# One MLP layer by seven block products instead of eight, in a two-layer hybrid inference step

## The chip, the core and the metric

The kernel runs on one core of a Trainium2 chip. The core has four compute engines, each with its own instruction stream that is worked off in order: TensorE (PE in the profile; its weight loads are shown apart as PEld), VectorE (DVE), ScalarE (ACT) and GpSimd (POOL). Transfers from memory are issued by a fifth stream, SyncE (SP). The metric is the device time of one execution in microseconds (us); lower is better.

## What is computed

The kernel is one inference step of a model with two layers (DEPTH = 2) over 640 tokens: 512 latent tokens and 128 context tokens, each with its own modulation vectors. Everything is float32. Each layer mixes tokens by four head groups and then runs a squared-ReLU MLP with 1024 features and 4096 hidden units:

```python
def squared_relu_mlp(h, w1, w2):
    return jnp.square(jax.nn.relu(h @ w1)) @ w2

def modulate(x, g, shift, scale):
    return rmsnorm(x, g) * (1 + scale) + shift

def trunk_layer(x, mod, p, mix_fn):
    shift1, scale1, gate1, shift2, scale2, gate2 = jnp.split(mod, N_MOD, axis=-1)
    y, ctx_state = mix_fn(modulate(x, p['norm1'], shift1, scale1))
    x = x + gate1 * y
    x = x + gate2 * squared_relu_mlp(modulate(x, p['norm2'], shift2, scale2), p['w1'], p['w2'])
    return x, ctx_state
```

The vectors in `mod` are products of the two groups' conditioning vectors with a weight matrix of 1024 by 6144 per layer; the kernel calls this part "ada".

## The kernel before

Features lie on the 128 partitions and tokens on the free axis, in two halves of 384 and 256 tokens (`HALVES`). Each float32 operand is held as a high and a low part, and every product is three matmuls: high by high, high by low, low by high (`mm3`, L241 to L243).

**Weights.** `load_unit` (L228) brings a unit of [128, 1024] floats: SP issues a transfer of 512 KB into one of three `raw` buffers, ACT casts it to the high part of one of four `hl` buffers (L232), and VectorE subtracts to get the low part (L233). With `pool=True` GpSimd does that subtraction; the first MLP uses it for the four units of its first block.

**MLP.** The 4096 hidden units are 32 tiles of 128. `mlp1(j)` makes four of them: for each tile and half, eight steps over the features, three matmuls each, so 192 matmuls. `mlp1_tile` (L1059) then takes the ReLU on ACT (L1067, `rr`), its square on GpSimd (L1068, `rq`), the square's high part on ACT (L1069, `u`) and the low part on VectorE (L1070). `mlp2(j)` multiplies the four tiles into eight output tiles, again 192 matmuls, and `gate_add` (L386) adds each result to `x` on VectorE. The order of the calls is mlp1(j+1), then mlp2(j), for j = 0 to 7; one such pair is called a cycle below.

**Ada steps.** `ada_tile` (L161) loads 512 KB into a `raw` buffer (`adaw`) and runs two custom VectorE instructions over it (L167, outputs `junk` and `adaw`), each followed by a short read of an accumulator (`mod`). 80 tiles are wanted by the end of layer 0; 56 of them are spread over layer 0's MLP by `ada_steps`, eight in most of its cycles. Layer 1's MLP has none.

**Start of an MLP.** After the out-projection the normalised, modulated operand is made by `Modulate` (L334): one VectorE instruction (L350), one on ACT (L357), one on VectorE (L358) for each feature tile and group of tokens. Its factor 1/rms (`rb`) needs a small power on GpSimd (L288, `nst`). The first half's eight steps run beside the end of the out-projection, the second half's after the first matmuls of `mlp1(0)`.

A scheduler fixes each engine's order ahead of time; buffer reuse becomes waits.

## Time and profile before

| | |
|---|---|
| median of 3 runs | 1563.75 us (1561.65 to 1564.59) |
| span of the profiled execution, first to last instruction | 1557.7 us |
| TensorE busy | 1491.2 us, 96% of the span, 9884 matmuls |
| VectorE busy | 1034.4 us, 66% |
| ScalarE busy | 612.0 us, 39% |
| GpSimd busy | 293.3 us, 19% |
| granted TensorE clock, mean | 0.984 of full |

The profiled execution is shown by its span; the timed runs' median lies 6.05 us above it. The busy shares are means over parts of the program with different loads: the MLP of layer 0 fills VectorE far more than that of layer 1, since the ada steps are in it.

### The profile page before, as it was taken

What the parts mean: (1) busy time and instruction counts of PE and PEld (TensorE: products, weight loads), DVE (VectorE), ACT (ScalarE), POOL (GpSimd) and SP (SyncE); (2) the same over time, 40 slices, a digit from 0 to 9 for tenths busy, and PEclk for the clock granted to TensorE, in tenths of its full rate; (3) what the DMA queues carried; (4) which work ended last, traced back from release to release, by engine and by line L of the source; (5) the groups of instructions that cost most, each with busy time, mean ns of one, the idle gap of its engine ahead of it and who ended that gap; (6) DMA issues with size and microseconds to landing.
All of it is one profiled execution on the core that took longest, in us unless ns stands there. A gap on an engine that the chain in (4) does not pass through costs nothing. (4 is left out here: it accounts for less than half of the span.)

```text
span 1557.7 us, 25473 instructions
## 1 busy us (share of the span) xinstructions
PE 1491.2 (96%) x9884; PEld 1434.7 (92%) x9884; DVE 1034.4 (66%) x2051; ACT 612.0 (39%) x1324; POOL 293.3 (19%) x309
## 2 busy tenths in 40 slices
...
GB/s 309 197 136 138 99 71 45 90 87 111 184 161 162 145 151 151 149 148 137 75 48 70 116 42 35 28 72 63 87 69 82 68 82 69 81 76 74 78 45 68
DMA packets 49816, 159.52 MB, mean 102 GB/s; under 512 B 6176, under 2 KB 10272, under 8 KB 49696
## 3 DMA queue, kind: packets, MB, share of 16 engines
...
q8 instruction: 78, 1.28, 0.3%
q14 instruction: 42, 0.34, 0.1%
...
## 5 line engine op out<-in xcount | busy, mean ns | idle before, releaser
L232 ACT CAST hl<-raw 128x1024 fp32r<-128x1024 f32 (+3 forms) x204 | 200.1, 983 | 400.4 <-PE w L243 320.1
L242 PE MATMUL w<-h,hl 128*128 128x256 f32 (+1 forms) x1024 | 317.3, 311 | 6.6 <-DVE h L358 6.6
L241 PE MATMUL w<-u,hl 128*128 128x384 f32 (+1 forms) x1024 | 317.4, 310 | 3.6 <-DVE x L386 3.5
L243 PE MATMUL w<-h,hl 128*128 128x256 f32 (+1 forms) x1024 | 317.9, 310 | 0.0
L243 PE MATMUL w<-u,hl 128*128 128x384 f32 (+1 forms) x1024 | 317.0, 310 | 0.0
L242 PE MATMUL w<-u,hl 128*128 128x384 f32 (+1 forms) x1024 | 316.9, 309 | 0.0
L241 PE MATMUL w<-h,hl 128*128 128x256 f32 (+1 forms) x1024 | 316.7, 310 | 0.0
L233 DVE TENSOR_TENSOR hl<-raw,hl 128x1024 fp32r<-128x1024 f32 (+3 forms) x184 | 216.0, 1176 | 106.4 <-ACT hl L232 106.1
L1068 POOL TENSOR_TENSOR rq<-rr 128x384 f32<-128x384 f32 (+1 forms) x128 | 110.0, 860 | 676.3 <-ACT rr L1067 629.3
L386 DVE SCALAR_TENSOR_TENSOR x<-w,mod,x 128x128 f32<-128x128 f32 (+1 forms) x384 | 154.8, 434 | 109.7 <-PE w L243 109.0
L242 PEld LDWEIGHTS w<-h,hl 128*128 128x128 f32 x1024 | 195.0, 190 | 8.3 <-DVE h L358 8.2
L241 PEld LDWEIGHTS w<-u,hl 128*128 128x128 f32 x1024 | 194.2, 190 | 4.5 <-DVE x L386 4.1
L243 PEld LDWEIGHTS w<-h,hl 128*128 128x128 f32 x1024 | 195.0, 190 | 0.0
L241 PEld LDWEIGHTS w<-h,hl 128*128 128x128 f32 x1024 | 194.9, 190 | 0.0
L242 PEld LDWEIGHTS w<-u,hl 128*128 128x128 f32 x1024 | 194.4, 190 | 0.0
L243 PEld LDWEIGHTS w<-u,hl 128*128 128x128 f32 x1024 | 194.2, 190 | 0.0
L167 DVE CUSTOM_DVE_ANT_0 junk<-adaw,cb,vec 128x1024 f32<-128x1024 f32 x84 | 115.3, 1373 | 65.5 <-DMA adaw<-in_wada 65.5
L1067 ACT ACTIVATE rr<-w 128x384 f32<-128x384 f32 (+1 forms) x128 | 55.9, 436 | 250.2 <-PE w L243 250.2
L1070 DVE TENSOR_TENSOR u<-rq,u 128x384 fp32r<-128x384 f32 (+1 forms) x128 | 67.8, 530 | 92.7 <-POOL rq L1068 92.6
L167 DVE CUSTOM_DVE_ANT_0 adaw<-adaw,cb,vec 128x1024 f32<-128x1024 f32 x84 | 115.1, 1370 | 1.3
L241 PE MATMUL fm<-h,hl 128*128 128x256 f32 (+1 forms) x288 | 92.2, 320 | 2.1 <-DVE u L533 2.1
L242 PE MATMUL fm<-h,hl 128*128 128x256 f32 (+1 forms) x288 | 90.0, 313 | 0.0
...
## 6 DMA issues: line engine op xcount, KB each, us to landing
raw<-in_wf SPq DMA_DIRECT2D x146, 512.0 KB, 3.5
adaw<-in_wada SPq DMA_DIRECT2D x84, 512.0 KB, 3.8
...
adan<-in_wnat SPq DMA_DIRECT2D x12, 512.0 KB, 8.4
...
raw<-in_wo SPq DMA_DIRECT2D x4, 512.0 KB, 3.7
```

Source lines behind the costliest of these rows:

```text
L167: nc.vector.tensor_tensor_reduce(out=raw if g else junk, in0=raw, in1=cb[:, g, :], op0=ALU.mult, op1=ALU.add, scale=1.0, scalar=vecs[l][:, ...
L232: nc.scalar.copy(hl[:, 0, :n], raw[:, :n])
L233: (nc.gpsimd if pool else nc.vector).tensor_sub(hl[:, 1, :n], raw[:, :n], f(hl[:, 0, :n]))
L241: nc.tensor.matmul(out, lhsT=lhs[0], rhs=rhs[0], start=start, stop=False)
L242: nc.tensor.matmul(out, lhsT=lhs[0], rhs=rhs[1], start=False, stop=False)
L243: nc.tensor.matmul(out, lhsT=lhs[1], rhs=rhs[0], start=False, stop=stop)
L386: nc.vector.scalar_tensor_tensor(out=x[:, m, t0:t0 + n], in0=ps[:, t0 - b0:t0 - b0 + n], scalar=mods[l][g][:, gate + m:gate + m + 1], in1= ...
L1067: nc.scalar.activation(r, ps[:, :n], AF.Relu)
L1068: nc.gpsimd.tensor_mul(q, r, r)
L1070: nc.vector.tensor_sub(ui[:, 1, t0:t0 + n], q, f(hh))
```

## The change

`mlp1` is replaced by pairs of hidden tiles (`Pair`), sixteen in a layer. A pair's weights are four blocks (two by two, features by hidden units), the operand four blocks of 512 features by 320 tokens (`HT`). Strassen's scheme forms seven products from sums of weight blocks and sums of operand blocks. A product is four feature steps of three matmuls over 320 columns, so a pair is 84 matmuls of 320 columns where before two tiles had 96, half of 384 and half of 256 columns.

The four weight sums are made by GpSimd (lines 1163 to 1166 of the new file) in buffers `s`; each pair then needs three and a half units cast and split instead of two: the first unit as it is, two units of sums, and one block of the second, whose low part GpSimd makes (line 1153 with `pool`). The results are put together by five VectorE additions from PSUM (`V`, `W` and three into `rr`), then ReLU, squares and split over 640 columns. `Blocks` takes the place of `Modulate` for this norm: it makes the seven operands; `t3`, the last sum and the low parts of `t3` and `t4` are GpSimd's (16 instructions of 320 columns), and the second half's steps go by `K_PAIRS`.

The order of calls becomes: pairs 0 and 1 interleaved at the start, then pair 2j+2, mlp2(j), pair 2j+3. Memory is shared by the phases of a layer (`open_phase`); so the masks and the rotary table are loaded anew in each layer, and the custom instruction's `junk` goes to a buffer in SBUF instead of PSUM while the MLP runs.

```diff
+K_PAIRS = (0, 4, 1, 5, 2, 6, 3, 7)
...
+    def open_phase(name, **pools):
+        phase["stack"] = ExitStack()
+        for key, bufs in pools.items():
+            phase[key] = phase["stack"].enter_context(
+                tc.tile_pool(name=f"{key}_{name}", bufs=bufs, reuse_waits="tile"))
+    def close_phase():
+        phase.pop("stack").close()
...
-        junk = bank2("junk").rearrange("p a b -> p (a b)")
+        if "me" in phase:
+            junk = phase["me"].tile([128, D], BF16, tag="junk", bufs=1, name=nm("junk"))
+        else:
+            junk = bank2("junk").rearrange("p a b -> p (a b)")
...
+        def put(self, op, s, src, pool=False):
+            o = self.op[op][s]
+            nc.scalar.copy(o[:, 0, :], src)
+            (nc.gpsimd if pool else nc.vector).tensor_sub(o[:, 1, :], src, f(o[:, 0, :]))
+        def step(self, half, k):
+            if k == 0:
+                self.rb[half] = self.norm.rstd(half)
+                for op in (("b11", "b21") if half == 0 else ("t2", "t3", "t1", "t4", "b22")):
+                    self.make(op)
+            z, s = divmod(k, 4)
+            if half == 0 and z == 0:
+                self.hf[s] = tb([128, 2, TOK], "hf", F32)
+            hf = self.hf[s]
+            b0 = HALVES[half][0]
+            for t0, n, g in REGIONS[half]:
+                nc.vector.scalar_tensor_tensor(
+                    out=hf[:, z, t0:t0 + n], in0=x[:, k, t0:t0 + n], scalar=gains[self.l][g][1][:, k:k + 1],
+                    in1=self.rb[half][:, t0 - b0:t0 - b0 + n], op0=ALU.mult, op1=ALU.mult)
+            for t0, n, g in REGIONS[half]:
+                nc.scalar.activation(hf[:, z, t0:t0 + n], hf[:, z, t0:t0 + n], AF.Identity,
+                                     bias=mods[self.l][g][:, 24 + k:25 + k])
+            if half == 0:
+                self.put(("b11", "b21")[z], s, hf[:, z, :HT])
+            elif z == 1:
+                b11, b12, b21, b22 = hf[:, 0, :HT], hf[:, 0, HT:], hf[:, 1, :HT], hf[:, 1, HT:]
+                t3, t2_ = tmp2([128, HT], "t3"), tmp2([128, HT], "t2")
+                nc.gpsimd.tensor_sub(t3, b12, b22)
+                nc.vector.tensor_sub(b12, b11, b12)
+                nc.vector.tensor_add(t2_, b22, b12)
+                self.put("t2", s, t2_)
+                self.put("t3", s, t3, True)
+                self.put("t1", s, b12)
+                nc.gpsimd.tensor_sub(b21, b21, t2_)
+                self.put("t4", s, b21, True)
+                self.put("b22", s, b22)
...
+        wide = tt([128, 768], "wide", F32)
+        nc.sync.dma_start(out=wide, in_=masks)
+        msk = lay.tile([128, 768], BF16, tag="msk", name=nm("msk"))
+        nc.vector.tensor_copy(msk, wide)
+        rq = lay.tile([128, TOK], F32, tag="rq", name=nm("rq"))
+        nc.sync.dma_start(out=rq, in_=rope_q)
...
+            def load(self):
+                self.raw = []
+                for i in range(2):
+                    raw = rawp.tile([128, 2, 512], F32, tag="raw", name=nm("raw"))
+                    nc.sync.dma_start(out=raw, in_=wf[l, U_W1 + 2 * self.p + i].rearrange("p (a b) -> p a b", a=2))
+                    self.raw.append(raw)
+            def hl(self, src, n=2, pool=False):
+                t = hlp.tile([128, 2, 2, 512], F32R, tag="hl", name=nm("hl"))
+                nc.scalar.copy(t[:, 0, :n], src)
+                (nc.gpsimd if pool else nc.vector).tensor_sub(t[:, 1, :n], src, f(t[:, 0, :n]))
+                return t
+            def w1(self):
+                self.wa = self.hl(self.raw[0])
+            def w2(self):
+                r1, r2 = self.raw
+                s23 = me.tile([128, 2, 512], F32, tag="s", bufs=3, name=nm("s"))
+                s14 = me.tile([128, 2, 512], F32, tag="s", bufs=3, name=nm("s"))
+                nc.gpsimd.tensor_add(s14[:, 0], r2[:, 0], r2[:, 1])
+                nc.gpsimd.tensor_add(s23[:, 0], r1[:, 0], s14[:, 0])
+                nc.gpsimd.tensor_add(s23[:, 1], r1[:, 0], r2[:, 0])
+                nc.gpsimd.tensor_add(s14[:, 1], r1[:, 1], s23[:, 0])
+                self.ws23 = self.hl(s23)
+                self.ws14 = self.hl(s14)
+                self.w22 = self.hl(r2[:, 1:2], 1, True)
...
+            def mul(self, ps, w, i, op, start):
+                for s in range(4):
+                    c = slice(128 * s, 128 * s + 128)
+                    b = mod.op[op][s]
+                    mm3(ps, (w[:, 0, i, c], w[:, 1, i, c]), (b[:, 0, :], b[:, 1, :]), start and s == 0, s == 3,
+                        not start)
...
+            def first(self):
+                self.a = bank("qa")[:, :HT]
+                self.mul(self.a, self.wa, 0, "b11", True)
+                self.q1 = me.tile([128, HT], F32, tag="q1", bufs=1, name=nm("q1")) \
+                    if self.p != 1 else tmp2([128, HT], "q1")
+                nc.scalar.copy(self.q1, self.a)
...
+            def second(self):
+                self.mul(self.a, self.wa, 1, "b21", False)
+                self.r[0] = tp([128, TOK], "rr")
+                nc.scalar.activation(self.r[0][:, :HT], self.a, AF.Relu)
+            def square(self, i):
+                r, u = self.r[i], self.u[i]
+                q = tp([128, TOK], "rq")
+                nc.gpsimd.tensor_mul(q, r, r)
+                nc.scalar.activation(u[:, 0, :], r, AF.Square)
+                nc.vector.tensor_sub(u[:, 1, :], q, f(u[:, 0, :]))
+            def rest(self, second):
+                bv = bank("qb")[:, :HT]
+                cd = bank2("qcd")
+                c, d = cd[:, 0, :HT], cd[:, 1, :HT]
+                self.mul(bv, self.ws23, 0, "t2", True)
+                v, w = tmp2([128, HT], "V"), tmp2([128, HT], "W")
+                nc.vector.tensor_sub(v, bv, self.q1)
+                self.mul(c, self.ws23, 1, "t3", True)
+                nc.vector.tensor_add(w, c, v)
+                if second:
+                    self.second()
+                self.mul(d, self.ws14, 0, "t1", True)
+                r0, r1 = self.r[0], tp([128, TOK], "rr")
+                self.r[1] = r1
+                nc.vector.tensor_sub(r1[:, HT:], w, d)
+                self.mul(c, self.w22, 0, "t4", False)
+                nc.vector.tensor_add(r1[:, :HT], c, v)
+                nc.scalar.activation(r1, r1, AF.Relu)
+                self.square(1)
+                self.mul(d, self.ws14, 1, "b22", False)
+                nc.vector.tensor_sub(r0[:, HT:], d, v)
+                nc.scalar.activation(r0[:, HT:], r0[:, HT:], AF.Relu)
+                self.square(0)
...
+        def full(p):
+            x_ = Pair(p)
+            x_.load()
+            x_.w1()
+            x_.w2()
+            x_.first()
+            x_.rest(True)
+            if l == 0:
+                ada_steps(4 if p == 2 else 2)
+            return x_.u
...
-        prev = mlp1(0)
+        us = []
+        head = [Pair(p) for p in range(2)]
+        for x_ in head:
+            x_.load()
+            x_.w1()
+            x_.first()
+            x_.second()
+            x_.w2()
+            if x_.p == 0:
+                for k in K_PAIRS:
+                    mod.step(1, k)
+        for x_ in head:
+            x_.rest(False)
+            us += x_.u
+            if l == 0:
+                ada_steps(2)
         for j in range(8):
-            cur = prev
             if j < 7:
-                prev = mlp1(j + 1)
-            mlp2(j, cur)
-    # ---------------- the step ----------------
+                us += full(2 * j + 2)
+            mlp2(j, us[4 * j:4 * j + 4])
+            if j < 7:
+                us += full(2 * j + 3)
+        close_phase()
```

On GpSimd, where an MLP starts (layer 1), the order before was the low parts of the first block's weights (L233), the power for the second half's 1/rms (`nst`), then the squares of the first tiles (`rq`):

```order
L233 TENSOR_TENSOR hl_11462<-raw_11460,hl_11462 128x1024
L233 TENSOR_TENSOR hl_11467<-raw_11465,hl_11467 128x1024
L233 TENSOR_TENSOR hl_11472<-raw_11470,hl_11472 128x1024
L288 TENSOR_TENSOR nst_11509<-nst_11509,mhalf 128x2
L1068 TENSOR_TENSOR rq_11501<-rr_11500 128x384
L1068 TENSOR_TENSOR rq_11596<-rr_11595 128x384
```

In the change the same place reads: the low part of pair 0's single block (`hl`), `nst`, the four sums of pair 1 (`s` from `raw`), and only then the operand work of the second half (`t`, `hf`, `ht`, rows of lines 431, 437 and 407, of which eleven more follow):

```order
L1153 TENSOR_TENSOR hl_11528<-raw_11482,hl_11528 128x512
L298 TENSOR_TENSOR nst_11534<-nst_11534,mhalf 128x2
L1163 TENSOR_TENSOR s_11682<-raw_11647 128x512
L1165 TENSOR_TENSOR s_11681<-raw_11645,raw_11647 128x512
L1164 TENSOR_TENSOR s_11681<-raw_11645,s_11682 128x512
L1166 TENSOR_TENSOR s_11682<-raw_11645,s_11681 128x512
L431 TENSOR_TENSOR t_1779_11557<-hf_11365 128x320
L431 TENSOR_TENSOR t_1781_11581<-hf_11409 128x320
L437 TENSOR_TENSOR hf_11365<-hf_11365,t_1780_11558 128x320
L407 TENSOR_TENSOR ht_1771_11541<-t_1779_11557,ht_1771_11541 128x320
L407 TENSOR_TENSOR ht_1775_11545<-hf_11365,ht_1775_11545 128x320
```

Where the weights' low parts and the squares stood, four sums of a later pair now stand ahead of the sixteen operand instructions.

On VectorE in layer 0's MLP, while mlp1 runs, the order before was, for each hidden tile, one ada tile (`junk`, `adaw`), one weight unit (L233) and two low parts of `u`:

```order
L233 TENSOR_TENSOR hl_4909<-raw_4907,hl_4909 128x1024
L1070 TENSOR_TENSOR u_4546<-rq_4683,u_4546 128x256
L167 ISA junk_5042,mod_123<-adaw_5040,cb,vec_99 128x1024
L167 ISA mod_123 128x1
L167 ISA adaw_5040,mod_123<-adaw_5040,cb,vec_99 128x1024
L167 ISA mod_123 128x1
L1070 TENSOR_TENSOR u_4547<-rq_4724,u_4547 128x384
L177 SCALAR_TENSOR_TENSOR gain_128<-mod_123,vec_99 128x1
L177 SCALAR_TENSOR_TENSOR gain_130<-mod_123,vec_99 128x1
```

While a pair runs in the change, the order is as follows; `V`, `W` and `rr` (lines 1204 to 1214) each wait for a product, and the weight units of the next pair (line 1153) stand between them:

```order
L177 ISA junk_6423,mod_115<-adaw_6421,cb,vec_93 128x1024
L177 ISA mod_115 128x1
L1153 TENSOR_TENSOR hl_6294<-raw_6290,hl_6294 128x1024
L177 ISA adaw_6421,mod_115<-adaw_6421,cb,vec_93 128x1024
L177 ISA mod_115 128x1
L1212 TENSOR_TENSOR rr_6240<-W_6199,qcd_6185 128x320
L1153 TENSOR_TENSOR hl_6303<-s_6297,hl_6303 128x1024
L177 ISA junk_6428,mod_115<-adaw_6426,cb,vec_93 128x1024
L177 ISA mod_115 128x1
L1214 TENSOR_TENSOR rr_6240<-qcd_6185,V_6198 128x320
L1153 TENSOR_TENSOR hl_6306<-s_6298,hl_6306 128x1024
```

Two ada tiles and three weight units stand among the additions of one pair.

At the start of layer 0's MLP, the ada tiles of pairs 0 and 1 stand among their additions, ahead of VectorE's part in the first mlp2. Before, the ada steps began with the second block of four tiles. Ten rows of the change:

```order
L177 ISA adaw_3935,mod_114<-adaw_3935,cb,vec_92 128x1024
L177 ISA mod_114 128x1
L177 ISA junk_4022,mod_114<-adaw_4020,cb,vec_92 128x1024
L177 ISA mod_114 128x1
L1212 TENSOR_TENSOR rr_3892<-W_3865,qcd_3851 128x320
L177 ISA adaw_4020,mod_114<-adaw_4020,cb,vec_92 128x1024
L177 ISA mod_114 128x1
L1204 TENSOR_TENSOR V_3954<-qb_3940,q_628_3819 128x320
L177 ISA junk_4027,mod_114<-adaw_4025,cb,vec_92 128x1024
L177 ISA mod_114 128x1
```

Of these ten rows two are additions of pairs; four are custom instructions of 1024 columns.

## Rows read from the trace of the kernel before

**Rows 1.** The page's first part: busy time, share of the span, instructions of each engine.

```profile
PE 1491.2 (96%) x9884; PEld 1434.7 (92%) x9884; DVE 1034.4 (66%) x2051; ACT 612.0 (39%) x1324; POOL 293.3 (19%) x309
```

**Rows 2.** Windows over the MLP of layer 0 (first column the stretch).

```profile
core 0: us, PE busy (x) PEld busy (x) DVE busy (x) ACT busy (x) POOL busy (x), PEclk, DMA share, GB/s
345.24:392.50 47.26, 42.44 (x283) 41.02 (x282) 45.32 (x83) 22.85 (x48) 16.95 (x14) 1.00 0.38 122
392.50:420.50 28.00, 24.45 (x168) 24.25 (x167) 26.48 (x39) 9.86 (x18) 8.62 (x6) 0.99 0.60 189
476.60:532.80 56.20, 56.20 (x384) 55.98 (x384) 43.84 (x81) 14.84 (x24) 7.71 (x8) 1.00 0.47 151
```

**Rows 3.** Windows, one cycle of layer 1's MLP, same columns.

```profile
1212.00:1268.00 56.00, 56.00 (x385) 56.00 (x384) 22.84 (x40) 14.80 (x24) 5.77 (x8) 1.00 0.23 75
```

**Rows 4.** Timeline of TensorE in layer 1's MLP: start, duration, line, operation; two block boundaries.

```profile
1200.32 0.34 PE L241 MATMUL w<-h,hl 128*128 128x384 f32 x1
...
1204.48 0.28 PE L241 MATMUL w<-h,hl 128*128 128x256 f32 x1
...
1207.35 0.34 PE L241 MATMUL w<-u,hl 128*128 128x384 f32 x1
```

**Rows 5.** Timeline of VectorE in layer 0's MLP, while mlp2 runs.

```profile
540.03 1.29 DVE L167 CUSTOM_DVE_ANT_0 junk<-adaw,cb,vec 128x1024 f32<-128x1024 f32 x1 [1.66 <-DMA adaw<-in_wada]
...
541.76 1.28 DVE L167 CUSTOM_DVE_ANT_0 adaw<-adaw,cb,vec 128x1024 f32<-128x1024 f32 x1
542.97 1.13 DVE L386 SCALAR_TENSOR_TENSOR x<-w,mod,x 128x384 f32<-128x384 f32 x3
544.02 1.21 DVE L233 TENSOR_TENSOR hl<-raw,hl 128x1024 fp32r<-128x1024 f32 x1
545.15 0.61 DVE L386 SCALAR_TENSOR_TENSOR x<-w,mod,x 128x384 f32<-128x384 f32 x1
```

**Rows 6.** Groups by line and form, layer 1's MLP: busy us, mean ns, idle before.

```profile
L1068 POOL TENSOR_TENSOR rq<-rr 128x384 f32<-128x384 f32 x24 | 19.8, 827 | 256.4 <-ACT rr L1067 234.8 <-issue 21.7
L1068 POOL TENSOR_TENSOR rq<-rr 128x256 f32<-128x256 f32 x25 | 15.4, 614 | 48.4 <-ACT rr L1067 48.4
L1070 DVE TENSOR_TENSOR u<-rq,u 128x384 fp32r<-128x384 f32 x25 | 14.0, 559 | 72.2 <-POOL rq L1068 72.2
L1070 DVE TENSOR_TENSOR u<-rq,u 128x256 fp32r<-128x256 f32 x25 | 10.4, 418 | 0.0
```

**Rows 7.** Timelines of GpSimd, VectorE and TensorE where layer 1's MLP starts, by time.

```profile
1067.36 4.31 POOL L263 TENSOR_TENSOR ss<-ss,sq 128x384 f32<-128x384 f32 x4 [0.61 <-ACT sq L262]
1087.58 0.34 PE L241 MATMUL w<-h,hl 128*128 128x384 f32 x1
1088.54 2.35 POOL L233 TENSOR_TENSOR hl<-raw,hl 128x1024 fp32r<-128x1024 f32 x1 [0.44 <-ACT hl L232]
1088.84 2.47 DVE L358 SCALAR_TENSOR_TENSOR h<-mt,mod,h 128x384 fp32r<-128x384 f32 x1
1091.36 0.45 PE L242 MATMUL w<-h,hl 128*128 128x384 f32 x1 [2.39 <-DVE h L358]
1092.27 0.60 DVE L358 SCALAR_TENSOR_TENSOR h<-mt,mod,h 128x384 fp32r<-128x384 f32 x1
1093.35 2.37 POOL L233 TENSOR_TENSOR hl<-raw,hl 128x1024 fp32r<-128x1024 f32 x1 [2.46 <-ACT hl L232]
```

**Rows 8.** Timelines of GpSimd and VectorE in layer 0's MLP, while mlp1 runs.

```profile
566.67 0.83 POOL L1068 TENSOR_TENSOR rq<-rr 128x384 f32<-128x384 f32 x1 [3.27 <-issue]
566.72 1.86 DVE L167 CUSTOM_DVE_ANT_0 junk<-adaw,cb,vec 128x1024 f32<-128x1024 f32 x1 [2.91 <-DMA adaw<-in_wada]
```

**Rows 9.** Timeline of TensorE where layer 0's MLP starts: the wait for half 1.

```profile
357.77 0.71 PE L290 MATMUL rb<-ident,nst 128*128 128x128 f32 x4 [1.03 <-POOL nst L288]
```

**Rows 10.** The list of waits over the span: us in total, times, longest us.

```profile
DVE junk L167 <- DMA adaw<-in_wada: 65.5, 47, 3.0
```

**Rows 11.** The page's list of transfers: count, KB each, median us from issue to landing.

```profile
raw<-in_wf SPq DMA_DIRECT2D x146, 512.0 KB, 3.5
```

83 lines of the change are left out of this document (35 added, 48 removed).

## The prediction

> **What bounds the kernel now.** I read the page's busy shares first: TensorE works 96% of the span [rows 1], so time comes off only where TensorE gets less work or the other engines can keep it fed. The windows over the MLP say where that is. In layer 0 a cycle (one mlp1, one mlp2: 384 matmuls) lasts 56.2 us, all of it TensorE's; VectorE is busy 43.84 us of it and GpSimd 7.71 [rows 2]. In layer 1, without the ada steps, VectorE has 22.84 us and GpSimd 5.77 [rows 3]. So VectorE has 12 us to spare in a cycle of layer 0 and 33 us in layer 1. The profiled span is 6.05 us under the runs' median; I add differences to the median. Less than 0.2% (3.1 us) cannot be told from no change.
>
> **What TensorE gives up.** In the timeline 24 matmuls of 384 columns take 1200.32 to 1204.48, 173.3 ns each, and 24 of 256 take 1204.48 to 1207.35, 119.6 ns each [rows 4]. On the line between them, 320 columns cost 146.5 ns. Each layer loses 16 x 12 = 192 matmuls: 192 x 146.5 = 28.1 us, 3.5 us per cycle, 56.2 us in all. That is the most that the change can bring, 3.6%. A cycle would be 360 x 146.5 ns = 52.7 us. The seven products use the same three-matmul form, so this term is firm.
>
> **What the other engines get, per cycle (two pairs).** Spacing of starts on VectorE: 1.21 us for a custom instruction (541.76 to 542.97), 1.13 for a weight unit (544.02 to 545.15), 0.08 less than the unit's own 1.21 [rows 5]. A low part of `u` of 384 or 256 columns takes 559 or 418 ns [rows 6]; less the same 0.08 that puts 320 columns at 0.41 us and 640 at 0.75. Removed: four weight units and eight low parts of `u`, 4 x 1.15 + 3.2 = 7.8 us. Added: 2 x (3 x 1.15 + 5 x 0.41 + 2 x 0.75) = 14.0. VectorE goes from 43.8 to 50.0 us in a cycle of layer 0, against TensorE's 52.7: 95% full, and to 29 us in layer 1.
>
> GpSimd's squares take 827 ns for 384 columns and 614 for 256 [rows 6], which puts 640 at 1.27 us. No weight sum is in the trace. The nearest rows are its two-input adds, 4.31 us for four of 384, and a subtraction of 1024 in 2.35 us [rows 7]; between them 512 columns cost 1.3 us, and on the same line 320 cost 0.95. A cycle's ten such instructions and four squares make 2 x (5 x 1.3 + 2 x 1.27) = 18 us, against 5.8 now. By itself that fits in 52.7 us.
>
> **It does not stand by itself.** At 1088.54 GpSimd starts a subtraction of 2.35 us; at 1088.84 VectorE starts an instruction that normally takes 0.60 us (1092.27), and it takes 2.47, ending 0.42 us after GpSimd; TensorE stands still for 2.39 us behind it [rows 7]. In the middle of layer 0's MLP the same: a custom instruction beside a square takes 1.86 us instead of 1.29 [rows 5, 8]. The blocking goes both ways: the same eight squares keep GpSimd 7.71 us in a cycle of layer 0 and 5.77 in one of layer 1 [rows 2, 3]. So what GpSimd and VectorE read from SBUF is worked off one after the other.
>
> The Trainium skill, "SBUF — State Buffer", section "Who interferes with whom", states the rule: a VectorE instruction with two SBUF inputs and a GpSimd instruction that reads SBUF use one shared port, and the second is fully blocked. The trace agrees, 2.47 against 0.60 us. It speaks against sums on GpSimd beside a full VectorE; without the rule the sum would be the first rival's.
>
> In a cycle of layer 0, VectorE's instructions with two SBUF inputs are ten weight units, four low parts and sixteen custom ones: 11.5 + 3.0 + 19.4 = 33.9 us, 68% of its 50.0. The additions and the `x` updates read PSUM with one input and can run beside GpSimd. If GpSimd's 18 us find VectorE at random, 68% of them, 12 us, lengthen the chain; if they always fall beside the PSUM readers, 2 us do. And both wait in order: VectorE for a product before each addition, and for the ada transfers, which already cost it 65.5 us in 47 waits [rows 10], with three `raw` buffers of which a pair now holds two until the sums are done. **I take 60.0 us for a cycle, nearer the random case** (bounds 53 and 67): five cycles with eight ada tiles lose 5 x 3.8 = 19 us. The sixth, with four tiles, and the last part are TensorE's and gain 3.5 + 1.7 = 5.
>
> **Start of layer 0's MLP.** Now the span from 345.24 to 392.50 holds 6 hidden tiles' work, 42.4 us, and 4.8 us of waits [rows 2]. In the change VectorE must work off, before the first mlp2's weights: the second half's operand (16 pieces of 0.26 and 20 of 0.41 us: 12.4), six weight units (6.9), eight ada tiles (16 x 1.32 with the accumulator reads: 21.1) and three pairs' additions and low parts (8.2 less or more): 48.6 us. It can begin when `rb` of the second half is there, 358.5 now [rows 9]; its `nst` now stands behind four sums and a low part on GpSimd (6.4 us, partly hidden), so I take 363. Without blocking that ends at 411.6, 19 us later than now. GpSimd has about 28 us in the stretch (nine sums and low parts of 1.3, sixteen of 0.95, the squares partly); one after the other with VectorE's 37 us of two-input work it ends at 426, 33.5 later. Since nearly every VectorE instruction there has two SBUF inputs, I take **+31**. The first mlp2 (now 28.0 us with 24.45 of TensorE [rows 2]) has 33 us of VectorE's work: **+5**. Layer 0: 31 + 5 + 19 - 5 = **+50 us** (bounds 0 and +85).
>
> **Start of layer 1's MLP.** No ada steps here. But GpSimd goes in order: the four sums of pair 1 need its second unit, whose transfer (3.5 us [rows 11]) starts only when a `raw` buffer of pair 0 is free. That is when pair 0's sums and single block are done, about 1095, near where GpSimd now has its last weights' low part (1093.35, 2.37 us [rows 7]); so the sums of pair 1 end near 1104, and the sixteen operand instructions behind them take 15 us alone, to 1119, or to 1126 if VectorE's 20 two-input pieces go between. TensorE has five of fourteen products left when the last piece of `t4` comes, about 9 us. With 1122 it ends the two pairs at 1131.5; two blocks' worth now ends at 1118.1 (1087.58 + 2.4 of waits + 28.1 [rows 7]). That is 13 us later where the saving alone would make it 3.5 earlier; with 1.5 us for pair 2's units, which queue behind, **18 us of layer 1's 28.1 are lost**. Later cycles have VectorE at 29 of 52.7 us: I allow 2 us in all. Layer 1: -28.1 + 18 + 2 = **-8 us** (bounds -18 and +2).
>
> The other edits cost nothing that the path sees: the masks and table are reloaded in layer 1 behind weight transfers that TensorE is not waiting for (0.7 MB, some 5 us at 512 KB in 3.5 [rows 11]; exposed, that would be the price), and `junk` in SBUF is written, not read.
>
> **Sum.** 1563.75 + 50 - 8 = **1605.8**; I say 1605.
>
> **Rivals.**
> *TensorE stays the bound (faster).* If VectorE's units run beside the sums without blocking, as the rows of 0.60 and 1.13 us do when GpSimd is idle, cycles of layer 0 are 52.7 (-17), its start costs 19 + 3, the tail gives 5, and layer 1 keeps 28.1 - 13: 1563.75 + 0 - 15 = about 1549. It decides itself at a cycle of 56.2 us: under 6 us of blocking per cycle, layer 0 stops losing outside its start. Against it stand [rows 7, 8]. 16%.
> *Only the starts pay.* The blocking fits into VectorE's PSUM pieces, cycles take 53.5: 1605 - 5 x 6.5 = 1573. For it: GpSimd's 18 us and VectorE's 34 still go into 52.7 with 1 us to spare. Against: neither waits for its turn only once. 22%.
> *VectorE and GpSimd saturate.* Cycles of 66 us, every sum blocked and the transfers late: 1605 + 5 x 6 = 1635. For it: transfer waits of up to 3.0 us, already now. 15%.
> *My forecast*, 1585 to 1620: 47%.
>
> **Chances.** Faster by over 0.2%: the first rival, 16%. Within 0.2%: the gap between the first two, 4%. Slower: 80%. The range reaches from 1556, which leaves out most of the first rival (12%), to 1632 (8%).
>
> **What would show it.** Matmuls of 320 columns 146 ns apart; cycles of layer 0 at 58 to 62 us with TensorE waiting for VectorE, VectorE over 93% busy and GpSimd over 18 us; weight units on VectorE well over 1.2 us while sums run; TensorE 15 to 25 us idle in the first 45 us of layer 1's MLP, waiting for GpSimd's `ht` rows. Wrong: cycles under 54 us in layer 0, weight units at 1.2 us beside sums, or a start whose stalls stay under 8 us.

## The result, and the profile after

The changed kernel takes 1655.19 us (median of 4 runs, 1650.13 to 1662.04) against 1563.37 us for the kernel before beside it (1561.65 to 1564.59): ratio 1.0585, 95% interval 1.055 to 1.0621. It is slower, as forecast, but by 92 us where 41 were forecast, and outside the range. The span of the profiled execution is 1652.5 us, 94.8 more than before, at a mean granted clock of 0.953 (0.984 before).

The page's first part, as [rows 1]: TensorE has 384 matmuls fewer and is busy only 5.6 us less, not 56.

```profile
PE 1485.6 (90%) x9500; PEld 1406.9 (85%) x9500; DVE 1195.3 (72%) x2196; ACT 687.3 (42%) x1380; POOL 535.0 (32%) x429
```

The span's 94.8 us, stage by stage, in us; "start" is the stretch from the out-projection's end until six hidden tiles are through mlp1:

| stage | before | after | difference | forecast |
|---|---|---|---|---|
| up to layer 0's MLP | 345.4 | 342.3 | -3.1 | 0 |
| start of layer 0's MLP | 48.9 | 79.5 | +30.6 | +31 |
| rest of layer 0's MLP | 415.7 | 462.3 | +46.6 | +19 |
| between the MLPs (mixing of layer 1) | 277.6 | 283.9 | +6.3 | 0 |
| start of layer 1's MLP | 49.5 | 69.8 | +20.3 | +12.7 |
| rest of layer 1's MLP, to the end | 420.7 | 414.7 | -5.9 | -20.8 |

In the change the start is counted to the first matmul of mlp2, with one product (layer 0) or two (layer 1) of pair 2 still to come. Before, six tiles are mlp1(0) and half of mlp1(1), and mlp2 starts two tiles later. The rows of TensorE's timeline before at which the seventh tile starts in layer 0, mlp2 starts there, and the seventh tile starts in layer 1:

```profile
394.32 0.34 PE L241 MATMUL w<-h,hl 128*128 128x384 f32 x1
408.39 0.34 PE L241 MATMUL w<-u,hl 128*128 128x384 f32 x1
1137.04 0.34 PE L241 MATMUL w<-h,hl 128*128 128x384 f32 x1
```

The forecast's 12.7 is its 13 us, with 1.5 for pair 2's units and less 1.8 that the third pair saves. Where the 3.1 us ahead of layer 0's MLP come from I did not look for.

**Layer 0.** Six intervals from one mlp2's first matmul to the next one's are 61.6, 64.1, 64.9, 64.0, 65.4 and 64.0 us (56.2 to 56.8 before, and 61.6 for the first). The windows below are the start of the MLP, the first of those cycles and two stretches of a cycle's length that begin later in an mlp2; columns as in [rows 2].

```profile
342.30:421.81 79.51, 49.27 (x249) 42.85 (x247) 69.47 (x108) 35.63 (x73) 40.85 (x32) 0.81 0.26 82
421.81:483.43 61.62, 54.23 (x349) 52.63 (x350) 51.38 (x81) 17.92 (x24) 21.46 (x14) 0.97 0.45 143
683.76:747.75 63.99, 58.01 (x363) 57.13 (x362) 55.03 (x95) 18.54 (x24) 21.20 (x15) 0.92 0.42 135
747.75:812.70 64.95, 56.70 (x362) 54.91 (x361) 50.47 (x75) 19.16 (x25) 20.99 (x15) 0.95 0.39 127
```

TensorE idles 7.4, 6.0 and 8.3 us of these cycles and is busy 54 to 58, where 360 matmuls at full clock are 52.7. VectorE is busy 50 to 55 us: 78 to 86%, so it does not saturate. How TensorE then comes to wait is in the timelines of VectorE, GpSimd and TensorE, by time, in layer 0's cycle around 720 us:

```profile
719.25 0.49 DVE L1206 TENSOR_TENSOR W<-qcd,V 128x320 f32<-128x320 f32 x1 [1.20 <-PE qcd L253]
721.59 1.73 DVE L177 CUSTOM_DVE_ANT_0 junk<-adaw,cb,vec 128x1024 bf16<-128x1024 f32 x1 [1.86 <-DMA adaw<-in_wada]
722.20 2.24 POOL L1164 TENSOR_TENSOR s<-raw,s 128x512 f32<-128x512 f32 x1
723.26 2.27 DVE L1153 TENSOR_TENSOR hl<-raw,hl 128x1024 fp32r<-128x1024 f32 x1
724.52 2.15 POOL L1166 TENSOR_TENSOR s<-raw,s 128x512 f32<-128x512 f32 x1
725.55 2.21 DVE L1153 TENSOR_TENSOR hl<-s,hl 128x1024 fp32r<-128x1024 f32 x1
725.58 0.41 PE L253 MATMUL qa<-hb,hl 128*128 128x320 f32 x1 [2.56 <-DVE hl L1153]
727.68 0.48 DVE L1212 TENSOR_TENSOR rr<-W,qcd 128x320 f32<-128x320 f32 x1
728.21 0.63 PE L251 MATMUL qcd<-ht,hl 128*128 128x320 f32 x1 [1.20 <-DVE rr L1212]
```

VectorE waits 1.86 us for a transfer of an ada tile, with the weight unit that TensorE needs behind it. The unit then takes 2.27 us beside two sums of 2.24 and 2.15 (1.21 alone [rows 5]), and TensorE waits 2.56 us for it. The addition into `rr` has a second slow unit ahead of it, and TensorE waits 1.20 us more. One late transfer and two blocked units make nearly 4 us.

TensorE does not wait for additions alone. Over the six cycles its list of waits has 18.2 us for the low part of a pair's first unit, 15.3 for additions, 9.1 for `x` updates and 2.9 for the units of mlp2. And what VectorE stands at longest is not the ada transfer (18.4 us in 13 waits) but the cast of a weight sum (33.5 us in 12), and GpSimd, which makes the sums, stands 117.4 us for the pairs' second units (22.8 us in layer 1's MLP from 1245 to 1600 us). Two rows of the list of waits from 424 to 812 us (us in total, times, longest), and one case in the timelines of GpSimd, ScalarE and VectorE:

```profile
POOL s L1163 <- DMA raw<-in_wf: 117.4, 12, 19.5
DVE hl L1153 <- ACT hl L1152: 33.5, 12, 4.6
```

```profile
700.83 1.29 POOL L1163 TENSOR_TENSOR s<-raw 128x512 f32<-128x512 f32 x1 [12.21 <-DMA raw<-in_wf]
705.63 1.05 ACT L1152 CAST hl<-s 128x1024 fp32r<-128x1024 f32 x1 [6.43 <-POOL s L1164]
706.71 1.33 DVE L1153 TENSOR_TENSOR hl<-s,hl 128x1024 fp32r<-128x1024 f32 x1 [3.50 <-ACT hl L1152]
```

The transfer is late for GpSimd's sum, the sum for the cast, the cast for VectorE; the `x` update stands behind that unit, and TensorE waits 2.23 us for it at 708.62. The pairs' transfers wait in turn for a `raw` buffer: in SyncE's list over the six cycles 58.5 us in 14 waits end with VectorE's last read of an ada tile.

A stall also costs afterwards. TensorE's timeline behind a wait of 2.23 us, by start:

```profile
708.62 0.44 PE L251 MATMUL w<-u,hl 128*128 128x384 f32 x1 [2.23 <-DVE x L447]
...
709.95 0.37 PE L252 MATMUL w<-u,hl 128*128 128x384 f32 x1
710.12 0.52 PE L253 MATMUL w<-u,hl 128*128 128x384 f32 x1
710.44 0.52 PE L251 MATMUL w<-u,hl 128*128 128x384 f32 x1
```

The matmuls start 170 ns apart up to 710.12 and 320 ns apart from there to 713.53: about half the rate, at a granted clock of 0.50, the lower of its two levels (1.2 against 2.4 GHz), for 3.4 us (0.99 in the 1.5 us ahead of it). That costs about 1.5 us more than the wait itself. In the six cycles the granted clock is at 0.50 in seven stretches, 44.4 us in all, each in or close behind one of TensorE's seven longest waits (2.23 to 5.28 us). At half the rate that is at most 22 us, 3.7 per cycle; TensorE is busy 56.4 us per cycle on average, 2.8 more than in layer 1's cycles at full clock (53.6).

**Start of layer 1's MLP.** Windows over it (TensorE idles 14.9 and 6.0 us, at granted clocks of 0.72 and 0.54), and below them the timelines of GpSimd, VectorE and TensorE:

```profile
1168.03:1190.30 22.27, 7.40 (x35) 6.20 (x34) 13.39 (x30) 11.86 (x27) 12.86 (x10) 0.72 0.13 47
1190.30:1210.00 19.70, 13.71 (x46) 11.13 (x46) 16.12 (x25) 10.22 (x28) 14.99 (x15) 0.54 0.09 28
```

```profile
1172.08 1.02 PE L293 MATMUL rb<-ones,ss 128*128 128x1 f32 x4 [3.76 <-DVE ss L273]
1173.61 4.67 POOL L1153 TENSOR_TENSOR hl<-raw,hl 128x512 fp32r<-128x512 f32 x1 [5.15 <-ACT hl L1152]
1181.90 1.27 POOL L1163 TENSOR_TENSOR s<-raw 128x512 f32<-128x512 f32 x1 [2.95 <-DMA raw<-in_wf]
1186.91 1.67 POOL L431 TENSOR_TENSOR t<-hf 128x320 f32<-128x320 f32 x2
1187.80 1.13 DVE L432 TENSOR_TENSOR hf<-hf 128x320 f32<-128x320 f32 x1 [5.44 <-POOL t L431]
1190.27 0.64 PE L251 MATMUL qb<-ht,hl 128*128 128x320 f32 x1 [8.54 <-ACT ht L406]
1200.14 0.63 PE L251 MATMUL qb<-ht,hl 128*128 128x320 f32 x1 [2.84 <-ACT ht L406]
```

In order: TensorE waits 3.76 us for the statistics; GpSimd's low part takes 4.67 us, with `nst` behind it; its first sum of pair 1 waits 2.95 us for its transfer; the four sums end at 1186.9; only then comes `t`, for which VectorE has waited 5.44 us; and TensorE waits 8.54 us for `t2`, made from it. That is the row of waits forecast, with longer links. The sums end 18.9 us into the start where 16.4 were forecast, and the last operand piece 41.0 us into it, at 1209.05, where 34.4 were forecast. TensorE has then done the work of six of the fourteen products of pairs 0 and 1, where nine were forecast.

**Between the MLPs.** A row of VectorE's timeline before, and the timelines of VectorE, GpSimd and TensorE in the change, where layer 1's mixing starts:

```profile
813.83 0.95 DVE L233 TENSOR_TENSOR hl<-raw,hl 128x768 fp32r<-128x768 f32 x1
```
```profile
887.95 0.55 DVE L461 CAST msk<-wide 128x768 bf16<-128x768 f32 x1
892.63 0.95 DVE L243 TENSOR_TENSOR hl<-raw,hl 128x768 fp32r<-128x768 f32 x1
892.72 1.43 POOL L298 TENSOR_TENSOR nst<-nst,mhalf 128x2 f32<-128x2 f32 x1 [7.40 <-DVE nsink L467]
894.20 1.04 PE L300 MATMUL rb<-ident,nst 128*128 128x128 f32 x4 [2.43 <-POOL nst L298]
```

TensorE waits 2.43 us for `nst` (0.28 before), although `nst` is not late: VectorE makes its input 8.4 us into this stage, 8.7 before. TensorE has run out of other work: 9 matmuls of the mixing stand between its two groups of `rb` matmuls, where 21 stood before. In VectorE's order the cast of the reloaded masks stands where a weight unit stood, and that unit now comes behind the statistics. That the reload is what moved the unit is argued from this order; no run took it away.

**Later cycles of layer 1** take 54.0 us where 52.7 were forecast, with TensorE busy and at full clock; 320-column matmuls start 147 ns apart (146.5 forecast). Below, the window of a cycle, and a row of TensorE's timeline whose wait, 0.43 us for `W`, comes back once in every cycle.

```profile
1244.77:1298.77 54.00, 53.57 (x362) 52.79 (x361) 31.92 (x48) 18.01 (x25) 20.76 (x15) 1.00 0.23 79
```

```profile
1290.97 0.41 PE L251 MATMUL qcd<-ht,hl 128*128 128x320 f32 x1 [0.43 <-DVE W L1206]
```

### The profile page after: what moved, and what is told of

Read it like the earlier page. It is cut to its first block, busy times and chain, and to the rows that moved or that the text cites. A ratio compares the mean times of both kernels' runs of the same rounds, so it can differ in the third digit from the quotient of the medians.

```text
span 1652.5 us, 24891 instructions
## 1 busy us (share of the span) xinstructions
PE 1485.6 (90%) x9500; PEld 1406.9 (85%) x9500; DVE 1195.3 (72%) x2196; ACT 687.3 (42%) x1380; POOL 535.0 (32%) x429
## 4 chain that ended last, share of the span: by engine, by line
PE 42%; DVE 4%; POOL 3%; issue 2%; ACT 2%; DMA 0%; POOLq 0%; DVEq 0%; ACTq 0%
PE w L252 5%; PE w L253 5%; PE w L251 5%; PE qcd L251 2%; PE qcd L252 2%; PE qcd L253 2%; PE fm L251 1%; PE qa L253 1%; PE fm L252 1%; PE fm L253 1%; PE qa L251 1%; PE qa L252 1%; PE tm L252 1%; PE tm L253 1%; PE tm L251 1%
## 5 line engine op out<-in xcount | busy, mean ns | idle before, releaser
L447 DVE SCALAR_TENSOR_TENSOR x<-w,mod,x 128x128 f32<-128x128 f32 (+1 forms) x384 | 152.6, 430 | 66.7 <-PE w L253 66.1
L1194 POOL TENSOR_TENSOR rq<-rr 128x640 f32<-128x640 f32 x64 | 103.1, 1611 | 300.6 <-ACT rr L1215 257.6
L242 ACT CAST hl<-raw 128x1024 fp32r<-128x1024 f32 (+3 forms) x140 | 133.2, 955 | 155.2 <-DMA raw<-in_wf 49.0
L243 DVE TENSOR_TENSOR hl<-raw,hl 128x1024 fp32r<-128x1024 f32 (+3 forms) x128 | 148.9, 1171 | 21.9 <-ACT hl L242 21.7
L251 PE MATMUL qcd<-ht,hl 128*128 128x320 f32 x384 | 127.2, 331 | 19.7 <-DVE W L1206 11.4
L177 DVE CUSTOM_DVE_ANT_0 junk<-adaw,cb,vec 128x1024 bf16<-128x1024 f32 (+1 forms) x84 | 117.5, 1399 | 19.2 <-DMA adaw<-in_wada 19.2
L1152 ACT CAST hl<-raw 128x1024 fp32r<-128x1024 f32 x64 | 53.4, 834 | 184.0 <-PE w L253 79.5
L252 PE MATMUL qcd<-ht,hl 128*128 128x320 f32 x384 | 123.6, 322 | 2.7 <-POOL ht L407 2.5
L253 PE MATMUL qcd<-ht,hl 128*128 128x320 f32 x384 | 122.7, 320 | 0.0
L1153 DVE TENSOR_TENSOR hl<-s,hl 128x1024 fp32r<-128x1024 f32 x64 | 82.7, 1295 | 51.6 <-ACT hl L1152 51.6
L1196 DVE TENSOR_TENSOR u<-rq,u 128x640 fp32r<-128x640 f32 x64 | 73.2, 1143 | 46.7 <-POOL rq L1194 46.7
L253 PE MATMUL qa<-hb,hl 128*128 128x320 f32 x256 | 85.0, 332 | 23.1 <-DVE hl L1153 23.1
L251 PEld LDWEIGHTS qcd<-ht,hl 128*128 128x128 f32 x384 | 75.9, 198 | 28.1 <-DVE W L1206 14.4
L251 PE MATMUL fm<-h,hl 128*128 128x256 f32 (+1 forms) x288 | 92.0, 320 | 2.1 <-DVE u L601 2.1
## 6 DMA issues: line engine op xcount, KB each, us to landing
raw<-in_wo SPq DMA_DIRECT2D x24, 384.0 KB, 3.0
raw<-in_wt SPq DMA_DIRECT2D x16, 384.0 KB, 3.4
```

What stands on the lines that cost most here:

```text
L177: nc.vector.tensor_tensor_reduce(out=raw if g else junk, in0=raw, in1=cb[:, g, :], op0=ALU.mult, op1=ALU.add, scale=1.0, scalar=vecs[l][:, ...
L242: nc.scalar.copy(hl[:, 0, :n], raw[:, :n])
L243: (nc.gpsimd if pool else nc.vector).tensor_sub(hl[:, 1, :n], raw[:, :n], f(hl[:, 0, :n]))
L251: nc.tensor.matmul(out, lhsT=lhs[0], rhs=rhs[0], start=start, stop=False, skip_group_check=more)
L252: nc.tensor.matmul(out, lhsT=lhs[0], rhs=rhs[1], start=False, stop=False, skip_group_check=more)
L253: nc.tensor.matmul(out, lhsT=lhs[1], rhs=rhs[0], start=False, stop=stop, skip_group_check=more)
```

## The experiments

All are edits of the changed kernel. One time stands for a single run beside the kernel before (1561 to 1565 us); where the ratio is given, repeated runs lie behind it. "Cycles" are the six intervals of layer 0 from mlp2 to mlp2, "starts" the stretches from an out-projection's end to the first mlp2: 79.5 and 69.8 us in the changed kernel. Its own four runs lie between 1650 and 1662 us, so a single time in that range does not tell an edit from the change, and most edits are read by their stages. Layer 1's start varies too: where its instructions are those of the change (the change itself, e2, e3, e7, e8, e14) it took 65.8 to 69.8 us.

**e1_no_sums**: what do the sums on GpSimd cost?

```diff
-                nc.gpsimd.tensor_add(s14[:, 0], r2[:, 0], r2[:, 1])
... (four sums)
-                self.ws23 = self.hl(s23)
-                self.ws14 = self.hl(s14)
+                self.ws23 = self.hl(r1)
+                self.ws14 = self.hl(r2)
```

> The four weight sums per pair are left out: the weights of t2, t3, t1 and b22 are cast and split from the two units as they come, so the products are not the reference's; all other work is as in the change. Changed kernel: 1655 us, cycles of layer 0 64.0 to 65.4 us, of layer 1 54.0. If GpSimd's sums block VectorE and that sets layer 0's cycle (my theory), cycles fall to about 56 us and the two starts by some 8 us each: about 1590 us. If the shared raw buffers and the ada transfers set it (rival), the pair's buffers come free only a few us earlier: cycles of 61 to 62, about 1630.

1620.38 us. Cycles 54.4, 60.1, 61.0, 57.9, 58.5, 59.0; starts 80.0 and 64.4. A window of a cycle:

```profile
600.13:657.99 57.86, 53.97 (x360) 52.74 (x360) 48.88 (x80) 18.03 (x25) 12.03 (x7) 1.00 0.46 146
```

Between the two. The sums, with the blocking, the waits for their casts and the longer hold on the `raw` buffers that come with them, cost about 5.5 us of a cycle (64.0 to 58.5) and 1 to 5 of layer 1's start; layer 0's start does not hang on them. Which of the three it is, this run does not separate.

**e2_ada_thin** and **e3_ada_no_load**: VectorE's ada work cut to 64 columns with the transfers kept, and the transfers taken away with the work kept (on a resident buffer).

```diff
+        w = 64 if "me" in phase else D
-                out=raw if g else junk, in0=raw, in1=cb[:, g, :], ...
+                out=(raw if g else junk)[:, :w], in0=raw[:, :w], in1=cb[:, g, :w], ...
```
```diff
+        if "me" not in phase:
             raw = pool(...)
             nc.sync.dma_start(out=raw, in_=wada[l, ct])
-                ... in0=raw, ...
+                ... in0=cb[:, 1 - g, :] if "me" in phase else raw, ...
```

> The two custom VectorE instructions of each ada tile in the MLP take 64 columns instead of 1024, so most of the modulation of layer 1 is not the reference's; the transfers of 512 KB stay. If VectorE's load together with the blocking sets layer 0's cycle (my theory), it falls to 54 to 55 us, as in layer 1, and the start of layer 0 by 15 us: about 1580 us. If the three raw buffers and the transfers set it (rival), cycles stay at 60 us or more: over 1615.

> The mirror of the run before: the ada tiles in the MLP keep their two custom VectorE instructions of 1024 columns with two SBUF inputs, but read a resident buffer; their transfers and raw buffers are gone, and the modulation of layer 1 is not the reference's. My theory (VectorE's load and the blocking): cycles of layer 0 stay at 60 us or more, over 1620 us. Rival (raw buffers and transfers): cycles of 54 to 56 us, 1590 us or less.

1618.05 us with the work cut: cycles 57.3 to 61.3, mean 59.8, starts 71.8 and 67.2. 1640.42 us without transfers: cycles 60.3 to 67.2, and 54.3 for the sixth, starts 70.7 and 65.9. Without transfers VectorE takes the tiles earlier: seven to ten in each of the first five cycles, where the change has eight, and none in the sixth. A window of each:

```profile
538.04:599.36 61.32, 54.32 (x363) 52.92 (x362) 34.72 (x81) 17.89 (x24) 20.51 (x14) 1.00 0.41 137
```

```profile
612.62:677.25 64.63, 56.74 (x361) 55.75 (x361) 57.90 (x103) 18.00 (x24) 26.64 (x14) 0.95 0.20 65
```

My theory, VectorE's amount of work, falls with the first window: VectorE is busy 35 of 61 us, the clock is full, and TensorE idles 7.0 us (3.3 to 5.1 in the other cycles). In that kernel VectorE's list of waits from 424 to 800 us still holds this row (us in total, times, longest), and one such wait, followed by TensorE's, stands in the timelines:

```profile
DVE junk L178 <- DMA adaw<-in_wada: 55.3, 26, 4.4
```

```profile
562.98 0.28 DVE L178 CUSTOM_DVE_ANT_0 junk<-adaw,cb,vec 128x64 bf16<-128x64 f32 x1 [4.43 <-DMA adaw<-in_wada]
...
563.94 0.36 PE L252 MATMUL w<-u,hl 128*128 128x256 f32 x1 [2.41 <-DVE x L448]
```

VectorE waits 4.43 us for a transfer; the `x` update behind that is late, and TensorE waits 2.41 us. Without transfers VectorE's 58 us and GpSimd's 26.6 (longer, by blocking) do the same, though with nearly ten tiles in that cycle; so e3 does not show what eight would do. So time is lost with the tiles' work cut away (e2), and with their transfers away at that higher load (e3).

**e8_no_ada** does both, leaving ada 64 columns of a resident buffer and no transfer.

> The ada tiles of the MLP are cut to 64 columns of a resident buffer, with no transfer (the modulation of layer 1 is not the reference's); all else as in the change. Taking away VectorE's part alone left cycles of 57 to 61 us, taking away the transfers alone 54 to 67. If the two together are what sets layer 0 apart, its cycles are layer 1's 54.0 and its start is layer 1's 70 us instead of 79.5: about 1585 us. If something else of layer 0 costs (rival), cycles stay over 56.

1602.02 us. Cycles 59.0, then 54.0 five times; starts 74.0 and 66.7.

```profile
592.64:646.64 54.00, 53.58 (x363) 52.80 (x361) 31.94 (x49) 18.01 (x24) 20.75 (x14) 1.00 0.25 79
```

With GpSimd's sums all in place, a cycle of layer 0 becomes one of layer 1, 54.0 us. VectorE is through with all the thin tiles by the end of the first cycle, so the other five hold none. Layer 0's start, 74.0, stays 4 us longer than expected. So the ada tiles (their waits, their work and the `raw` buffers they hold) set the cycle apart: thin tiles give back 4 us, no tiles 10; what the transfers alone give back stays open, since e3's cycles hold more tiles.

**e4_operands_dve**: the second half's GpSimd operands on VectorE. Is the order on GpSimd what makes the starts long?

```diff
-                nc.gpsimd.tensor_sub(t3, b12, b22)
+                nc.vector.tensor_sub(t3, b12, b22)
... (t4 and both low parts alike)
```

> The sixteen operand instructions at the start of each MLP go from GpSimd to VectorE; the results stay the reference's. In the change TensorE waits 8.54 us (layer 1) and 5.69 us (layer 0) for the first t2, behind the four sums of pair 1 on GpSimd. If GpSimd's order is the cause (my theory), these waits fall below 2 us, TensorE's clock does not drop there, and each start is 12 to 18 us shorter: about 1628 us. If the blocking between the two engines is the cause (rival), VectorE's sixteen more two-input instructions wait for the same sums and the starts change by less than 5 us each: 1645 to 1660.

1662.9 us; starts 78.2 and 70.0. The wait for `t2` fell from 8.54 to 2.90 us, another of 3.95 came behind it, and nothing was gained: the work is late on the one engine as on the other. The starts are as the rival had them.

**e12_no_t34** leaves GpSimd's 16 operand instructions out altogether.

```diff
-                nc.gpsimd.tensor_sub(t3, b12, b22)
-                self.put("t3", s, t3, True)
-                nc.gpsimd.tensor_sub(b21, b21, t2_)
-                self.put("t4", s, b21, True)
+                    self.op["t3"], self.op["t4"] = self.op["t1"], self.op["b22"]
```

> GpSimd's sixteen operand instructions at the start of each MLP are left out, with ACT's casts for t3 and t4: the products t3 and t4 take the operands of t1 and b22, so the result is not the reference's; the weight sums and everything later stay. If the amount of operand work that GpSimd and VectorE do one after the other sets the start (theory after the run with another order), both starts are 10 us or more shorter: layer 1's about 57 us instead of 66 to 70, the whole about 1633. If the wait is for the weight sums and VectorE's own chain (rival), they are 0 to 4 us shorter: 1647 or more.

1647.34 us; starts 72.6 and 62.3, cycles 61 to 68. Even all of GpSimd's operand work gone takes only 7 us off each start, and in layer 1 perhaps only 4, by the spread above. That lies between what the theory and the rival had.

**e5_two_banks**: the accumulators `c` and `d` in buffers of their own.

```diff
-                cd = bank2("qcd")
-                c, d = cd[:, 0, :HT], cd[:, 1, :HT]
+                c, d = bank2("qc")[:, 0, :HT], bank2("qd")[:, 0, :HT]
```

> The two accumulators c and d of a pair get a buffer each instead of the two halves of one; the results stay the reference's. As written, t1 (into d) waits until W has read c, t4 (into c) until the sum before it has read d, b22 likewise, so TensorE waits for VectorE's newest addition after each product. New theory: this handover, with VectorE working in order behind ada tiles and weight units, sets layer 0's cycle (7.6 us of TensorE's idle time in each, 3 to 4 us more by the lower clock after each). Then a product of slack more takes most of it away: cycles of 64.3 fall to 57 to 59, stalls to under 4, about 1620 us. Rival (VectorE and GpSimd are simply late with their work): cycles change by less than 2 us, 1643 to 1657.

1650.02 us. Cycles of layer 1 fell from 54.0 to 53.3, those of layer 0 did not (62.0 to 68.3): there the additions are late, not kept apart by a buffer.

**e6_fill**: 40 dummy matmuls ahead of layer 1's (and 0's) first `t2`. Is the start long because the clock drops while TensorE idles?

```diff
+        for n in range(40):
+            nc.tensor.matmul(fb, lhsT=head[1].wa[:, 0, 0, 0:128], rhs=mod.op["b11"][n % 4][:, 0, :], start=True, stop=True)
```

> Forty matmuls of 320 columns whose product nobody reads are put in front of the first t2 product of each MLP, where TensorE now waits 8.54 us (layer 1) and 5.69 us (layer 0); the results stay the reference's. If the lowered clock makes the starts long (theory: windows of 0.54 to 0.72 of the clock from 1168 to 1210 us), the granted clock there is near 1.00 after them and each start is 3 to 8 us shorter although TensorE does more: about 1643 us. If the chain of VectorE and GpSimd alone sets the end of the start (rival), the starts are the same within 2 us or longer by what the matmuls take at the low clock: 1653 to 1662.

1657.66 us; starts 79.8 and 66.7. The two windows that answer to those of layer 1's start above:

```profile
1175.98:1198.30 22.32, 15.71 (x77) 14.24 (x76) 17.24 (x33) 13.69 (x32) 12.18 (x12) 0.77 0.16 48
1198.30:1218.00 19.70, 13.67 (x58) 12.24 (x59) 16.29 (x27) 10.34 (x24) 13.22 (x13) 0.65 0.08 27
```

Twice the TensorE work went into the same 22.3 us: VectorE and GpSimd set that stretch, not TensorE. The granted clock rose only to 0.77 and 0.65, not to the 1.00 of the theory, so what a full clock would give is not shown. Layer 1's whole start is 3 us shorter, but within what equal code shows.

**e14_fill_cycles**: 24 dummy matmuls of 192 columns after `b21` in layer 0's pairs. Does idle time just take them in, or does a busier TensorE get its clock back?

```diff
+                if l == 0 and self.p > 1:
+                    for n in range(24):
+                        nc.tensor.matmul(self.qa[:, HT:], lhsT=self.wa[:, 0, 0, 0:128], rhs=mod.op["b11"][n % 4][:, 0, :192], start=True, stop=True)
```

> In each of layer 0's later pairs, 24 matmuls of 192 columns that nobody reads (about 90 ns each at the full clock, 4.3 us per cycle) stand between the product b21 and t1, where TensorE waits for W in the change; the results stay the reference's. If the lowered clock lengthens the cycle (theory: 58 us of TensorE's busy time in a cycle against 53.5 in layer 1), the granted clock rises and the cycle falls from 64 to 60 or 62 us although TensorE does 4 us more. If VectorE's work sets the cycle (rival), it stays at 64 us or grows by up to 4.

1733.19 us, which neither theory had. Cycles 74.4 to 78.3; TensorE idles 13 us in each, VectorE is busy 65% in the one below, and the clock is no better:

```profile
580.15:657.27 77.12, 63.51 (x410) 62.23 (x409) 50.20 (x80) 18.40 (x24) 21.87 (x14) 0.91 0.34 109
```

VectorE's timeline there: the last custom instruction of one ada tile, 3.64 us of waiting for the next tile's transfer, its first custom instruction, and some 3.7 us later the addition for which TensorE stands still.

```profile
578.63 1.28 DVE L177 CUSTOM_DVE_ANT_0 adaw<-adaw,cb,vec 128x1024 f32<-128x1024 f32 x1
583.56 1.28 DVE L177 CUSTOM_DVE_ANT_0 junk<-adaw,cb,vec 128x1024 bf16<-128x1024 f32 x1 [3.64 <-DMA adaw<-in_wada]
587.24 0.48 DVE L1217 TENSOR_TENSOR rr<-W,qcd 128x320 f32<-128x320 f32 x1
```

The cycle grows by 13 us for work that would take 4 at the full clock (48 x 87 ns, half of the 173 ns for 384 columns): more work in the same pair does not fill the idle time, it lengthens the cycle. That TensorE, VectorE and the transfers wait for each other in a loop is how I read it; the run shows the result, not the loop. What the clock alone costs stays open with it.

**e7_layer1_only**: layer 0 keeps the eight products, layer 1 has seven.

```diff
-        mod = Blocks(norm2, l)
+        mod = Blocks(norm2, l) if l else Modulate(norm2, l, 1)
... (layer 0: mlp1 and mlp1_tile of before)
```

> Layer 0 gets the first MLP layer and the Modulate of the kernel before, layer 1 the seven products; the phases and their buffers stay. The results stay the reference's. If the parts add up, layer 0 is as in the kernel before and what is left over it is layer 1's 14.7 us and some 3 us where the layers meet: about 1582 us. If layer 1 in the change suffered from what layer 0 left behind (rival), it is below 1570.

1571.97 us, 10.6 over the kernel before; layer 1's start 66.5, its cycles 54.0. So by this single run nearly nine tenths of the loss are layer 0's; the table above puts 74 of the 95 us up to the end of its MLP.

**e11_banks**: e7 with e5's edit. **e9_ordered** and **e10_ordered_banks**: e7, and e7 with e5's edit, with the order at the start written out.

```diff
+        with tc.issue_after(norm2.nst.ins):
+            head[0].split3(False)
+        with tc.issue_after(mod.last.ins):
+            head[1].sums()
+            head[1].split3(True)
```

> Seven products in layer 1 alone, as in the run layer1_only (1572 us), and at their start another order: on GpSimd the sums of pair 1 stand behind the sixteen operand instructions; on VectorE the low parts of pair 0's sums stand behind the statistics of the second half, and pair 0's single block is split there; the results stay the reference's. If the order in which the two engines work sets the length of the start (theory), it loses 6 to 10 us: about 1564. If the amount of their work does (rival), the start changes by less than 3 us: 1569 to 1574.

> As ordered, and the two accumulators of a pair in a buffer each, which took layer 1's cycles from 54.0 to 53.3 us and its last part down by 4: 6 x 0.7 + 4 = 8 us under the run before, 1556 us, the first version under the kernel before, if the two add up (theory). Rival: the later pairs' products run into the buffers that are now held longer, and it stays within 3 us of the run before.

> Layer1_only with the buffers alone, the start as in the change: 1572 - 8 = 1564 us if cycles and last part gain as they did with seven products in both layers; rival: 1569 to 1574.

| | median us | runs | ratio to before (95%) | layer 1's start | its cycles |
|---|---|---|---|---|---|
| e9_ordered | 1577.74 | 4 | 1.0092 (1.0074 to 1.011) | 72.9 | 54.0 |
| e10_ordered_banks | 1570.48 | 8 | 1.0047 (1.0029 to 1.0066) | 73.9 | 53.3, 52.7 |
| e11_banks | 1567.24 | 7 | 1.0013 (0.9991 to 1.0036) | 70.3 | 53.3 |

The order did not shorten the start, it took 72.9 us, longer than either theory or rival had. In e9 TensorE waits 3.60 us for `W`; VectorE had stood 5.69 us for a square of GpSimd's, which comes behind the sums of pair 2. My theory that GpSimd's order makes the start long fell here a second time. The two buffers help: e10 is 7.3 us under e9, where 8 were forecast. e11_banks is the best version that came out of this: no difference from the kernel before that can be told. Its 1567.24 lies between its theory and its rival.

## Why the prediction came out right in direction and wrong in size

**Held.** TensorE's saving per matmul (147 ns against 146.5). The blocking of VectorE by GpSimd: weight units of 2.27 and 2.21 us beside sums, 1.21 alone; e1 gives back 5.5 us of each cycle when the sums go. The rule of the Trainium skill, "SBUF — State Buffer", section "Who interferes with whom", agrees with these numbers, and it was right that it speaks against this change. The start of layer 0's MLP: +30.6 against +31, but partly by luck. I let VectorE begin at 363; `rb` of the second half was there at 354.1, and from there to the first mlp2 it took 67.7 us and not the 60.5 that I had. And the weight sums that I put into it are not needed: e1 leaves the start at 80.0, while e2 and e3 take 8 to 9 off it and e12 7. TensorE's idle time in a cycle of layer 0: 6 to 8 us, where 60.0 - 52.7 = 7.3 was forecast.

**Step that failed: "I take 60.0 us for a cycle", and the sixth and last "are TensorE's and gain 3.5 + 1.7".** Six intervals were forecast at 358 us (5 x 60.0, 5 for the first mlp2, 52.7) and took 384.0. Of these 26 us, 11 are the sixth: it has eight ada tiles like the others, and takes 64.0 like them. I had counted four, as before, and my 8 + 5 x 8 + 4 makes 52 of the 56 tiles. The other 15, 3 us per cycle, are TensorE being busy 54 to 58 us for 52.7 of work, with the granted clock at 0.50 in or behind its seven longest waits. I priced the stalls and not the clock that comes with them. That all 3 us would come back without the stalls is argued, not shown, for no experiment changed the clock alone.

**Its reason was half right.** "VectorE 95% full" and over 93% busy were forecast, 78 to 86% came. e2 shows that its amount of work is not needed for the loss: with VectorE busy 57 to 63% the cycles still took 59.8 us on average, 7 more than 52.7. e3 shows that the transfers aren't needed either, at a higher load of tiles. e8 shows that the ada tiles, sums and all else kept, are the whole difference from layer 1's cycle. How they do it I read from the rows: VectorE's queue is worked off in order, and units that wait for late sums (33.5 us), ada tiles that wait (18.4 us) and units that are blocked stand ahead of the units, additions and `x` updates for which TensorE waits. A wait for ada transfers does not cost by itself: before, VectorE stood 63.9 us in 44 such waits (420.5 to 757.6 us), and TensorE did not idle. That the pairs' transfers are late because pairs and ada tiles share three `raw` buffers fits SyncE's waits; no run changed the buffers alone.

**Step that failed: layer 1's start, "13 us later".** By my own end points it lasts 69.8 us where 57.4 were forecast. The kernel before was misread as well: I put the end of its fourth tile at 1118.1, the fifth starts at 1122.98 in the trace. Against the trace the start is 20.3 us longer than before. (The window of "the first mlp2 (now 28.0 us", behind +5, is misread too: mlp2 starts at 408.39, in its middle. And 363 + 28 + 37 is 428, not 426.) The row of waits is the one forecast; its links were too short. Of the 12.4 us the sums are 2.5, the operand work behind them 4.1; "five of fourteen products left" were eight, three products or 5.3 us more. GpSimd's low part took 4.67 us, not 1.3, before `nst`; the first statistics came 3.76 us late; and TensorE worked at granted clocks of 0.54 to 0.72 between its stalls. e4, e9 and e10 show that reordering only moves the wait, e12 that even GpSimd's operand work gone gives 4 to 7 us, e6 that TensorE's share of its first 22 us is not what sets them. That the start's work on VectorE and GpSimd as a whole, blocked by turns, is longer than TensorE's fourteen products is what is left; it is argued, not shown, and which link would have to go first stays open.

**Step that failed: the masks "cost nothing that the path sees".** The stage took 6.3 us more; that this is near the 5 that I had named as the exposed price is luck, since nothing waits for the reload itself. 3.9 of it lie in the first 66 us, with the wait of 2.43 at 894.20 and a granted clock of 0.97 there (1.00 before); the other 2.4 I could not place.

**Layer 1's later cycles** were mis-sized by 1.3 us each (54.0 for 52.7), 7.8 us where I allowed 2 in all: the handover of the two accumulators in one buffer is 0.7 of it (e5).

**The rivals.** "Only the starts pay" (cycles of 53.5) fell, "TensorE stays the bound" too. "Saturate" (66 us, 1635) was nearest in its number and half right in its mechanism: the transfers were late, but VectorE was not full, and not every sum was blocked (1478 to 1617 ns on average in layer 0's MLP, 1.29 us alone).
